# Gate and up of two feed-forward chunks as seven block products each, on one Trainium2 core

## The chip, the cores and the metric

The kernel runs on one core of one Trainium2 chip. The engines are named as the profile names them: PE (TensorE, matmul) with PEld (its weight loads), DVE (VectorE), ACT (ScalarE), POOL (GpSimd) and SP (SyncE, which issues the DMAs here). The metric is the device time of one execution in microseconds, less is better.

## The reference

Two layers, each with three sublayers (feed-forward, mixer, feed-forward), on 512 rows of 1024 channels. A modulation vector, one silu(c) @ ada_w per sublayer, shifts and scales the input of each sublayer and gates its output; a layer norm follows. Four of the six sublayers are the feed-forward network that the change touches:

```
def swiglu(h, w_gate, w_up, w_down):
    return (jax.nn.silu(h @ w_gate) * (h @ w_up)) @ w_down

def _ada_post_norm(x, mod, fn, ln_g, ln_b, res_w):
    shift, scale, gate = mod[:, 0, None], mod[:, 1, None], mod[:, 2, None]
    y = fn(x * (1 + scale) + shift)
    return layer_norm(DEEPNORM_ALPHA * x + res_w * (1 + gate) * y, ln_g, ln_b)
```

w_gate and w_up are 1024 x 2816, w_down is 2816 x 1024, all in 32-bit floating point.

## The kernel before

Channels lie on the 128 partitions, rows on the free axis: X, XH and XL are [128, 8, 512]. XH is the value rounded to the format of the matmul, XL the rest. Weights are split in the same way into a high and a low part, and each product of two values is three matmuls (high x high, high x low, low x high; `mm3`, L375 to L377).

Phases 0 to 5 are the sublayers: 0, 2, 3, 5 are feed-forward (FFN), 1 and 4 the mixers. An FFN works through its 2816 hidden channels in three chunks of 6, 8 and 8 tiles (`CHUNKS`). For each tile one **unit** is loaded: gate and up weights of 128 hidden channels, [128, 2, 8, 128], 1 MB. Gate and up are each 8 x 3 matmuls of 512 columns into one PSUM bank (PM, three banks). ACT takes silu out of PSUM (L644), DVE multiplies by up (L648), ACT casts the high part hH (L148), DVE forms the low part hL (L151). After a chunk's units comes its down stage: 8 output tiles, each evacuated by `resid` (L548, DVE), weights in four units. In chunks 0 and 1 it goes over all 512 columns; in chunk 2 (`last_projection`) first over one half of the columns for all output tiles, then over the other, and layer norm of the first half runs beside the second half of the products.

Units are handed through buffers. `load` fetches a unit into one of two raw buffers (SP). `halve` splits it in two steps, an ACT cast (L252) and, one piece later, a DVE subtraction (L255), into one of three buffers of the pool wp (tags wh, wl) or, for a few units, of the phase's own pool (tags dh, dl). `ready` lets a unit in only when the unit three before it (two for class d) has been marked done by `free`. `take` waits for a unit to be split and writes out what is still missing.

The order of work is written out by hand (`manual_schedule`): `run` emits a piece of matmuls with its evacuation, then `step` (what `after` has put off, as the DVE half of a split), then `tick`, which loads every fourth time, does a modulation sum every `ticks["ada"]` times, and else a halving on odd counts. Each engine executes its own queue in the order of emission. A modulation sum (`ada_sum`, L297) is one DVE operation over [128, 1024] after a 512 KB load into one of two aw buffers; there are 24 for each phase, 144 in all. `ADA_EVERY` sets their distance: one number for each phase, 3, 0, 6, 5, 0, 0. `ada_finish` does what is left of them and the small scalar operations (L322 to L334).

## Time and profile before

| | us |
|---|---|
| median of 3 runs | 1983.27 (1979.55 to 1985.62) |
| profiled execution, its own time | 1983.02 |
| its span, first to last instruction | 1981.2 |
| PE busy | 1950.2 |
| DVE busy | 1072.1 |
| ACT busy | 643.8 |

A row of the timeline gives the start, the duration, engine, line, operation, out<-in and shapes; a number in brackets is the idle time of the engine before it and what ended it. Matmuls overlap in their records, so the distance of two starts is what one costs. On DVE and ACT too an operation's record reaches some 0.08 us into the next one, so what one costs in a queue is again the distance of starts.

### The profile page before, as it was taken

What the parts mean: (1) busy time and instruction counts of PE and PEld (TensorE: products, weight loads), DVE (VectorE), ACT (ScalarE), POOL (GpSimd) and SP (SyncE); (2) the same over time, 40 slices, a digit from 0 to 9 for tenths busy, and PEclk for the clock granted to TensorE, in tenths of its full rate; (3) what the DMA queues carried; (4) which work ended last, traced back from release to release, by engine and by line L of the source; (5) the groups of instructions that cost most, each with busy time, mean ns of one, the idle gap of its engine ahead of it and who ended that gap; (6) DMA issues with size and microseconds to landing.
All of it is one profiled execution on the core that took longest, in us unless ns stands there. A gap on an engine that the chain in (4) does not pass through costs nothing.

```text
span 1981.2 us, 25603 instructions
## 1 busy us (share of the span) xinstructions
PE 1950.2 (98%) x10650; PEld 1659.7 (84%) x10650; DVE 1072.1 (54%) x1958; ACT 643.8 (32%) x966; POOL 0.3 (0%) x5
## 2 busy tenths in 40 slices
PE   7999999999999999999999999999999999999997
PEld 5888888988777998888899888888888998888887
DVE  7675654645356845545476545544795663333335
ACT  4322223253344532222335223122442352231221
POOL 0000000000000000000000000000000000000000
PEclk9999999999999999999999999999999999999998
DMA  9576652231141335444432554533122222323211
GB/s 340 199 266 231 212 191 92 75 107 64 54 138 65 112 123 181 154 165 149 160 127 85 174 188 160 180 107 128 65 86 85 86 96 97 107 85 106 86 64 43
DMA packets 57352, 259.18 MB, mean 131 GB/s; under 512 B 6083, under 2 KB 15724, under 8 KB 38549
## 3 DMA queue, kind: packets, MB, share of 16 engines
q1 hardware_dynamic: 57236, 257.56, 37.7%
q8 instruction: 83, 1.36, 0.3%
q14 instruction: 33, 0.26, 0.0%
HBM read 255.41 MB, written 2.12 MB: 130 GB/s over the span
## 4 chain that ended last, share of the span: by engine, by line
PE 94%; DVE 3%; DMA 1%; ACT 1%; issue 0%; SPq 0%; DVEq 0%; ACTq 0%
PE pm L375 30%; PE pm L376 29%; PE pm L377 29%; PE pa L1018 1%; PE pm L1042 1%; DMA aw<-in_adaw 1%; PE pb L485 1%; DVE aw L297 1%; PE pa L448 0%; ACT w L461 0%; PE pb L1029 0%; DVE wl L255 0%; PE pa L491 0%; DVE w L469 0%; DVE X L459 0%
## 5 line engine op out<-in xcount | busy, mean ns | idle before, releaser
L375 PE MATMUL pm<-XH,wh 128*128 128x512 f32 (+1 forms) x1656 | 619.0, 374 | 12.6 <-ACT wh L1306 11.6
L376 PE MATMUL pm<-XL,wh 128*128 128x512 f32 (+1 forms) x1656 | 614.5, 371 | 1.3 <-DVE XL L1354 1.3
L377 PE MATMUL pm<-XH,wl 128*128 128x512 f32 (+1 forms) x1656 | 614.2, 371 | 0.0
L255 DVE TENSOR_TENSOR wl<-raw,wh 128x1024 fp32r<-128x1024 f32 (+1 forms) x288 | 338.6, 1192 | 84.1 <-ACT wh L252 81.2
L252 ACT CAST wh<-raw 128x1024 fp32r<-128x1024 f32 (+1 forms) x288 | 285.0, 1024 | 280.4 <-PE pm L376 188.4
L375 PEld LDWEIGHTS pm<-XH,wh 128*128 128x128 f32 x1656 | 312.0, 188 | 73.5 <-ACT wh L1306 11.6
L376 PEld LDWEIGHTS pm<-XL,wh 128*128 128x128 f32 x1656 | 312.2, 189 | 60.1 <-DVE XL L1354 2.2
L377 PEld LDWEIGHTS pm<-XH,wl 128*128 128x128 f32 x1656 | 311.8, 188 | 59.4 <-DVE wl L1308 0.3
L648 DVE TENSOR_TENSOR w<-w,pm 128x512 f32<-128x512 f32 (+1 forms) x100 | 60.8, 608 | 382.4 <-PE pm L377 382.1
L376 PE MATMUL pm<-hL,wh 128*128 128x512 f32 (+1 forms) x704 | 250.8, 356 | 0.0
L375 PE MATMUL pm<-hH,wh 128*128 128x512 f32 (+1 forms) x704 | 250.2, 355 | 0.0
L377 PE MATMUL pm<-hH,wl 128*128 128x512 f32 (+1 forms) x704 | 247.7, 352 | 0.0
L548 DVE SCALAR_TENSOR_TENSOR X<-pm,sm,X 128x256 f32<-128x256 f32 (+1 forms) x176 | 101.4, 579 | 201.1 <-PE pm L377 201.1
L148 ACT CAST hH<-w 128x512 fp32r<-128x512 f32 (+1 forms) x103 | 57.6, 560 | 430.0 <-DVE w L648 430.0
L297 DVE CUSTOM_DVE_ANT_0 aw<-aw,sc_t,prm_t 128x1024 f32<-128x1024 f32 x144 | 183.6, 1280 | 24.2 <-DMA aw<-in_adaw 24.2
L375 PEld LDWEIGHTS pm<-hH,wh 128*128 128x128 f32 x704 | 132.2, 188 | 22.1
L377 PEld LDWEIGHTS pm<-hH,wl 128*128 128x128 f32 x704 | 132.4, 188 | 20.1
L376 PEld LDWEIGHTS pm<-hL,wh 128*128 128x128 f32 x704 | 132.4, 188 | 19.7
L644 ACT ACTIVATE w<-pm 128x512 f32<-128x512 f32 (+1 forms) x101 | 53.9, 534 | 202.1 <-PE pm L377 202.0
L151 DVE TENSOR_TENSOR hL<-w,hH 128x512 fp32r<-128x512 f32 (+1 forms) x103 | 63.3, 615 | 64.9 <-ACT hH L148 64.9
L375 PE MATMUL pm<-hH,dh 128*128 128x256 f32 x256 | 72.6, 284 | 0.0
L376 PE MATMUL pm<-hL,dh 128*128 128x256 f32 x256 | 72.4, 283 | 0.0
(239 smaller groups left out, 2143.0 us busy)
## 6 DMA issues: line engine op xcount, KB each, us to landing
raw<-in_wgu SPq DMA_DIRECT2D x84, 1024.0 KB, 4.9
aw<-in_adaw SPq DMA_DIRECT2D x144, 512.0 KB, 5.2
raw<-in_wd SPq DMA_DIRECT2D x32, 1024.0 KB, 5.0
raw<-in_wd SPq DMA_DIRECT2D x16, 768.0 KB, 4.2
raw<-in_abfm SPq DMA_DIRECT2D x8, 1024.0 KB, 4.8
raw<-in_cdfm SPq DMA_DIRECT2D x8, 1024.0 KB, 6.2
raw<-in_wgu SPq DMA_DIRECT2D x16, 256.0 KB, 8.9
raw<-in_abtm SPq DMA_DIRECT2D x4, 1024.0 KB, 4.9
```

The source lines that it names most:

```text
L148: A.copy(h, v)
L151: V.tensor_tensor(out=l, in0=v, in1=h.bitcast(F32), op=ALU.subtract)
L252: A.copy(u.hl[0][:, x], u.raw[:, x])
L255: V.tensor_tensor(out=u.hl[1][:, x], in0=u.raw[:, x], in1=u.hl[0][:, x].bitcast(F32), op=ALU.subtract)
L297: V.tensor_tensor_reduce(out=w, in0=w, in1=sc_t, scale=1.0, scalar=prm_t[:, c0:c0 + 1], op0=ALU.mult, op1=ALU.add, accum_out=mod[i][:, t:t ...
L375: T.matmul(ps, st[0], mv[0], start=first, stop=False)
L376: T.matmul(ps, st[0], mv[1], start=False, stop=False)
L377: T.matmul(ps, st[1], mv[0], start=False, stop=last)
L485: T.matmul(pv[t], q[:, n, t * P:(t + 1) * P], inv[:, 0:1], start=m + n == 0, stop=m == len(terms) - 1 and n == 1)
L548: V.scalar_tensor_tensor(out=X[:, d, cs], in0=ps, scalar=scal["G", i][:, d:d + 1], in1=X[:, d, cs], op0=ALU.mult, op1=ALU.add)
L644: A.activation(st["sg"], ps, AF.Silu)
L648: V.tensor_tensor(out=sg, in0=sg, in1=ps, op=ALU.mult)
```

## The change

In chunks 1 and 2 of each FFN, gate and up of a tile are computed together, as a product of 2 x 2 blocks with seven block products. The blocks are: of the weights, gate or up by the first or second four channel tiles (a11, a12, a21, a22); of the moving side, channel tiles 0 to 3 or 4 to 7 by the first or second 256 columns (HA, HB). Each block product is 4 x 3 matmuls of 256 columns. The products accumulate in three PSUM banks for each tile: product 1 is written to bank a and copied by ACT to bank b, in which product 2 adds to it; products 6, 7 and 4 add to bank a, with a copy or an addition taken out in between; product 5 is written to bank c, copied out, and product 3 adds to it. Product 4 of a tile is issued after products 1 and 5 of the next one. The two parts of ADA_EVERY, the waits and the buffers change with it:

- `quarter` takes the place of `halve` for these units: four sums and differences of weight blocks on DVE, four ACT casts, four DVE low parts; a unit takes two of the three wp buffers.
- `sums_of` forms the sums and differences of the moving blocks during the down stage of chunk 0, on DVE and ACT, into T23 and T4, which take the buffers of tags dh and dl until chunk 2's products are done, and over the second half of XH and XL for channel tiles 0 to 3.
- The down stage of chunk 2 keeps one unit of class d in place of two.
- Modulation sums: none in gate and up of chunks 1 and 2; every 4th tick in the down stage of chunk 0, every 2nd in those of chunks 1 and 2 (first half of columns); every 5th in the mixers. All later phases stand in one list from the start. `ada_finish` moves from before the first half of `last_projection` to behind it.

```
-ADA_EVERY = (3, 0, 6, 5, 0, 0)
+ADA_EVERY = {"up": (3, 0, 0, 0, 0, 0), "down": (4, 2, 2), "mixer": (0, 5, 0, 0, 5, 0)}
...
-                        add(wgu[f, j], [2, KT, P], "d" if j in ((3, 4) if i else (4,)) else "w", i)
+                        if c:
+                            add_seven(wgu[f, j], i)
+                        else:
+                            add(wgu[f, j], [2, KT, P], "d" if j in ((3, 4) if i else (4,)) else "w", i)
+                    if c == 0:
+                        hold(i)
                     for g in range(4):
-                        add(wd6[f, g] if n == 6 else wd8[f, c - 1, g], [2, n, P], "d" if c == 2 and g > 1 else "w", i)
+                        add(wd6[f, g] if n == 6 else wd8[f, c - 1, g], [2, n, P], "d" if c == 2 and g > 2 else "w", i)
...
+    def quarter(u):
+
+        sub = u.subs[u.n // 2]
+        if sub.hl is None:
+            if u.i not in sums_at or not ready(sub):
+                return False
+            sub.hl = tuple(wp.tile([P, 2, KT, P], F32R, tag="w" + x, name=nm("w" + x)) for x in "hl")
+        sr = sums_at[u.i]
+        a11, a12, a21, a22 = (u.raw[:, m, 4 * k:4 * k + 4, :] for m in range(2) for k in range(2))
+        if u.n == 0:
+            V.tensor_tensor(out=sr[:, 0], in0=a21, in1=a22, op=ALU.add)
+            V.tensor_tensor(out=sr[:, 1], in0=sr[:, 0], in1=a11, op=ALU.subtract)
+        elif u.n == 1:
+            V.tensor_tensor(out=sr[:, 2], in0=a11, in1=a21, op=ALU.subtract)
+            V.tensor_tensor(out=sr[:, 3], in0=a12, in1=sr[:, 1], op=ALU.subtract)
+        src = (u.raw[:, 0], sr[:, 0:2].rearrange("p a b c -> p (a b) c"), sr[:, 2:4].rearrange("p a b c -> p (a b) c"),
+               u.raw[:, 1, 4:8, :])[u.n]
+        h, l = (t[:, u.n % 2, 0:src.shape[1], :] for t in sub.hl)
+        u.n += 1
+        last = u.n == 4
+        A.copy(h, src)
+
+        def low():
+            V.tensor_tensor(out=l, in0=src, in1=h.bitcast(F32), op=ALU.subtract)
+            u.lows += 1
...
-        if ticks["n"] % 2 and halve():
+        if (eager or ticks["n"] % 2) and halve():
...
-        ada_finish(i + 1)
         zs = [W2([P, 2, HALF]) for _ in range(2)]
...
         for g in tiles(0):
             run(g)
+        ada_finish(i + 1)
...
+            def values():
+                for n in (k, k + 4):
+                    st[n] = W2()
+                    V.tensor_tensor(out=st[n], in0=XH[:, n, :].bitcast(F32), in1=XL[:, n, :].bitcast(F32), op=ALU.add)
+
+            def sums():
+                a, b = st[k], st[k + 4]
+                t, q = st["t"], st["q"] = W2([P, 2, HALF]), W2([P, 2, HALF])
+                V.tensor_tensor(out=q[:, 0], in0=a[:, HB], in1=a[:, HA], op=ALU.subtract)
+                V.tensor_tensor(out=t[:, 0], in0=b[:, HB], in1=q[:, 0], op=ALU.subtract)
+                V.tensor_tensor(out=t[:, 1], in0=b[:, HB], in1=a[:, HB], op=ALU.subtract)
+                V.tensor_tensor(out=q[:, 1], in0=b[:, HA], in1=t[:, 0], op=ALU.subtract)
+                A.copy(T23[0][:, k], t)
+                A.copy(XH[:, k, HB], q[:, 0])
+                A.copy(T4[:, 0, k], q[:, 1])
...
+                def e1(ps):
+                    A.copy(at("b")(), ps)
+
+                def e2(ps):
+                    t["g"] = W2()
+                    A.activation(t["g"][:, HA], ps, AF.Silu)
+                    free(u.subs[0])
+
+                def e3(ps):
+                    V.tensor_tensor(out=t["g"][:, HB], in0=t["u2"], in1=ps, op=ALU.add)
+                    A.activation(t["g"][:, HB], t["g"][:, HB], AF.Silu)
+
+                def e7(ps):
+                    t["c"] = W1()
+                    V.tensor_tensor(out=t["c"], in0=t["p5"], in1=ps, op=ALU.add)
+
+                def e4(ps):
+                    free(u.subs[1])
+                    g = t["g"]
+                    V.tensor_tensor(out=g[:, HA], in0=g[:, HA], in1=ps, op=ALU.mult)
+                    V.tensor_tensor(out=g[:, HB], in0=g[:, HB], in1=t["c"], op=ALU.mult)
+                    split(hH[:, jj, :], hL[:, jj, :], g)
...
+                p = unit(u, jj, (PM, PA)[jj % 2])
+                run([p[1], p[5]] + ([before[4]] if before else []) + [p[6], p[2], p[3], p[7]], eager=True)
+                before = p
+            run([before[4]], eager=True)
...
+            ticks["ada"] = ADA_EVERY["up"][i] if c == 0 else 0
+            if c:
+                seven(range(n), hH, hL)
+                jj = n
+                if c == len(CHUNKS) - 1:
+                    free(*held_d[i])
...
+                moving_sums = [f for k in range(4) for f in sums_of(k)]
...
+                        if c == 0:
+                            for f in moving_sums[3 * d // 2:3 * (d + 1) // 2]:
+                                after(1 + (d % 2), f)
```

## Rows read from the trace of the kernel before

**Rows 1.** The page's totals by engine, and TensorE's longest wait by who ended it: us in total, times, longest us.

```profile
PE 1950.2 (98%) x10650; PEld 1659.7 (84%) x10650; DVE 1072.1 (54%) x1958; ACT 643.8 (32%) x966; POOL 0.3 (0%) x5
...
PE pm L375 <- ACT wh L1306: 11.6, 1, 11.6
```

**Rows 2.** Busy time of each engine (instructions in brackets), granted clock, DMA share and GB/s in three stretches: gate and up of chunk 2 of the first FFN, the down stage of chunk 0 of the second FFN, and its down stage of chunk 2.

```profile
252.30:341.80 89.50, 89.50 (x389) 72.27 (x388) 40.20 (x48) 25.32 (x33) 0.00 (x0) 1.00 0.42 146
734.20:767.80 33.60, 33.60 (x146) 27.03 (x145) 19.74 (x25) 7.80 (x10) 0.00 (x0) 1.00 0.43 148
992.60:1041.00 48.40, 47.83 (x397) 47.55 (x397) 35.68 (x80) 15.93 (x24) 0.00 (x0) 1.00 0.36 122
```

**Rows 3.** Timeline of PE: the first and the seventh of a run of 512-column matmuls; the first and the thirteenth of a run of 256-column ones with weights in the pool of tag wh; the first and the tenth of a run with weights in that of tag dh.

```profile
303.10 0.39 PE L375 MATMUL pm<-XH,wh 128*128 128x512 f32 x1
304.50 0.39 PE L375 MATMUL pm<-XH,wh 128*128 128x512 f32 x1
...
705.93 0.28 PE L375 MATMUL pm<-XH,wh 128*128 128x256 f32 x1
707.29 0.28 PE L375 MATMUL pm<-XH,wh 128*128 128x256 f32 x1
...
690.02 0.28 PE L375 MATMUL pm<-XH,dh 128*128 128x256 f32 x1
691.10 0.29 PE L375 MATMUL pm<-XH,dh 128*128 128x256 f32 x1
```

**Rows 4.** Timeline, mostly of DVE, in several stretches: operations that follow each other without idle time, the end of a unit (last matmul, then the multiplication), and a pair of 512-wide additions of which the second reads the first.

```profile
208.06 0.69 DVE L151 TENSOR_TENSOR hL<-w,hH 128x512 fp32r<-128x512 f32 x1 [0.69 <-ACT hH L148]
208.67 1.28 DVE L297 CUSTOM_DVE_ANT_0 aw<-aw,sc_t,prm_t 128x1024 f32<-128x1024 f32 x1
...
733.85 0.40 PE L377 MATMUL pm<-XH,wl 128*128 128x512 f32 x1
734.36 0.69 DVE L648 TENSOR_TENSOR w<-w,pm 128x512 f32<-128x512 f32 x1 [7.46 <-PE pm L377]
...
764.37 1.22 DVE L255 TENSOR_TENSOR wl<-raw,wh 128x1024 fp32r<-128x1024 f32 x1
765.50 1.28 DVE L297 CUSTOM_DVE_ANT_0 aw<-aw,sc_t,prm_t 128x1024 f32<-128x1024 f32 x1
...
1046.69 1.42 DVE L469 TENSOR_TENSOR w<-w,w 128x512 f32<-128x512 f32 x2 [0.16 <-ACT w L461]
...
1061.96 0.75 DVE L510 TENSOR_TENSOR XL<-w,XH 128x256 fp32r<-128x256 f32 x2
```

**Rows 5.** Groups of instructions by line and shape, of ACT: busy us, mean ns of one, then idle time before them.

```profile
L252 ACT CAST wh<-raw 128x1024 fp32r<-128x1024 f32 x256 | 259.3, 1048 | 253.9 <-PE pm L376 188.4 <-issue 23.2 <-DMA raw<-in_wgu 19.9
L148 ACT CAST hH<-w 128x512 fp32r<-128x512 f32 x73 | 45.4, 622 | 380.2 <-DVE w L648 380.2
L644 ACT ACTIVATE w<-pm 128x256 f32<-128x256 f32 x30 | 11.5, 382 | 13.9 <-PE pm L377 13.8
```

**Rows 6.** The page's DMA issues: queue, count, KB each, median us from issue to landing.

```profile
raw<-in_wgu SPq DMA_DIRECT2D x84, 1024.0 KB, 4.9
aw<-in_adaw SPq DMA_DIRECT2D x144, 512.0 KB, 5.2
```

**Rows 7.** Timeline of DVE in the down stage of chunk 0 of the second FFN.

```profile
735.73 0.69 DVE L151 TENSOR_TENSOR hL<-w,hH 128x512 fp32r<-128x512 f32 x1 [0.69 <-ACT hH L148]
...
738.50 0.75 DVE L548 SCALAR_TENSOR_TENSOR X<-pm,sm,X 128x512 f32<-128x512 f32 x1 [1.07 <-PE pm L377]
739.17 0.95 DVE L255 TENSOR_TENSOR wl<-raw,wh 128x768 fp32r<-128x768 f32 x1
740.03 1.28 DVE L297 CUSTOM_DVE_ANT_0 aw<-aw,sc_t,prm_t 128x1024 f32<-128x1024 f32 x1
741.24 0.08 DVE L297 DVE_READ_ACCUMULATOR2_ANT mod<- 128x1 f32 x1
```

**Rows 8.** Timeline of DVE at the start of the down stage of chunk 0 of the first FFN, where PE begins at 83.28.

```profile
94.01 0.75 DVE L548 SCALAR_TENSOR_TENSOR X<-pm,sm,X 128x512 f32<-128x512 f32 x1
...
100.40 1.29 DVE L297 CUSTOM_DVE_ANT_0 aw<-aw,sc_t,prm_t 128x1024 f32<-128x1024 f32 x1 [2.05 <-DMA aw<-in_adaw]
...
106.80 1.28 DVE L297 CUSTOM_DVE_ANT_0 aw<-aw,sc_t,prm_t 128x1024 f32<-128x1024 f32 x1 [0.85 <-DMA aw<-in_adaw]
```

**Rows 9.** Timeline of PE at its start, and the table by stretches (columns as in rows 2) around its longest later wait, in the second mixer.

```profile
12.57 0.63 PE L377 MATMUL pm<-XH,wl 128*128 128x512 f32 x1
13.00 0.63 PE L375 MATMUL pm<-XH,wh 128*128 128x512 f32 x1
...
1424.00:1427.00 3.00, 0.99 (x9) 0.74 (x7) 2.81 (x5) 2.98 (x4) 0.00 (x0) 0.99 0.06 25
1427.00:1431.00 4.00, 4.00 (x13) 3.29 (x14) 3.68 (x19) 2.48 (x3) 0.00 (x0) 0.58 0.02 4
```

**Rows 10.** Timeline of DVE in the down stage of chunk 2 of the second FFN: the first evacuation of the second half, and the first operation of layer norm.

```profile
1017.82 0.48 DVE L548 SCALAR_TENSOR_TENSOR X<-pm,sm,X 128x256 f32<-128x256 f32 x1 [1.67 <-PE pm L377]
1018.68 2.48 DVE L459 TENSOR_TENSOR X<-X,pa 128x512 f32<-128x512 f32 x4 [0.38 <-PE pa L448]
```

**Rows 11.** Timeline of DVE at the start of the third FFN: the last low part of the first five units, and the multiplication of the fifth.

```profile
1064.78 1.22 DVE L255 TENSOR_TENSOR dl<-raw,dh 128x1024 fp32r<-128x1024 f32 x1
...
1071.48 0.42 DVE L648 TENSOR_TENSOR w<-w,pm 128x256 f32<-128x256 f32 x1 [2.24 <-PE pm L377]
```

More of the change, by code (lines that the diff above doesn't have):

```diff
@@ L163, in __init__ @@
             self.split = self.done = False
+            self.subs = None
+            self.n = self.lows = 0
     units = []
@@ L175, in add, with add_seven, hold @@
             members.setdefault((cls, i if cls != "w" else 0), []).append(u)
+        def add_seven(src, i):
+            u = Unit(src, [2, KT, P], "s", i)
+            u.subs = [Unit(None, u.shape, "w", i) for _ in range(2)]
+            units.append(u)
+            members.setdefault(("w", 0), []).extend(u.subs)
+        def hold(i):
+            held_d[i] = [Unit(None, None, "d", i) for _ in range(2)]
+            members.setdefault(("d", i), []).extend(held_d[i])
         for i in range(6):
@@ L261, in halve, with quarters @@
         return True
+    def quarter(u):
[21 more added lines that the diff above has]
+            u.lows += 1
+            if last:
+                u.split = True
+                halved[0] += 1
+        begun[0] += last
+        after(1, low)
+        return True
+    def quarters(u, n):
+        while u.lows < n:
+            if u.n >= n:
+                settle()
+            else:
+                assert load() or halve(), (used[0], halved[0], loaded[0], u.n)
     def prepare():
@@ L358, in tick, with run @@
             defer.pop(0)()
-    def run(pieces, extras=None, quiet=False):
+    def run(pieces, extras=None, quiet=False, eager=False):
         for n, p in enumerate(pieces):
@@ L366, in run @@
             if not quiet:
-                tick()
+                tick(eager)
     def flush(q):
@@ L632, in ffn, with sums_of, lows @@
         j0 = 0
+        T23 = T4 = None
+        def sums_of(k):
+            st = {}
+            def values():
[12 more added lines that the diff above has]
+                A.copy(T4[:, 0, k], q[:, 1])
+            def lows():
+                t, q = st["t"], st["q"]
+                for o, v, h in ((T23[1][:, k], t, T23[0][:, k]), (XL[:, k, HB], q[:, 0], XH[:, k, HB]),
+                                (T4[:, 1, k], q[:, 1], T4[:, 0, k])):
+                    V.tensor_tensor(out=o, in0=v, in1=h.bitcast(F32), op=ALU.subtract)
+            return values, sums, lows
@@ new lines, in seven, with product, piece, both @@
+        def seven(js, hH, hL):
+            def product(u, n, need, sub, w, ps, mv, first, evac):
+                def piece():
+                    quarters(u, need)
+                    h, l = u.subs[sub].hl
+                    ps_ = ps()
+                    for k in range(4):
+                        st_ = (h[:, w // 2, 4 * (w % 2) + k, :], l[:, w // 2, 4 * (w % 2) + k, :])
+                        m = mv(k)
+                        for x, (s_, v_) in enumerate(((st_[0], m[0]), (st_[0], m[1]), (st_[1], m[0]))):
+                            T.matmul(ps_, s_, v_, start=first and k + x == 0, stop=k == 3 and x == 2, skip_group_check=not first)
+                    evac(ps_)
+                return piece
+            def both(k, cs):
+                return XH[:, k, cs], XL[:, k, cs]
+            def unit(u, jj, bank):
+                b = {}
+                def at(n):
+                    def get():
+                        if n not in b:
+                            b[n] = bank([P, HALF])
+                        return b[n]
+                    return get
+                t = {}
+                def keep(n):
+                    def evac(ps):
+                        t[n] = W1()
+                        A.copy(t[n], ps)
+                    return evac
+                def e1(ps):
[16 more added lines that the diff above has]
+                    split(hH[:, jj, :], hL[:, jj, :], g)
+                p = {
+                    1: product(u, 1, 1, 0, 0, at("a"), lambda k: both(k, HA), True, e1),
+                    5: product(u, 5, 2, 0, 2, at("c"), lambda k: both(k, HB), True, keep("p5")),
+                    6: product(u, 6, 2, 0, 3, at("a"), lambda k: (T23[0][:, k, 0], T23[1][:, k, 0]), False, keep("u2")),
+                    2: product(u, 2, 1, 0, 1, at("b"), lambda k: both(4 + k, HA), False, e2),
+                    3: product(u, 3, 3, 1, 1, at("c"), lambda k: both(4 + k, HB), False, e3),
+                    7: product(u, 7, 3, 1, 0, at("a"), lambda k: (T23[0][:, k, 1], T23[1][:, k, 1]), False, e7),
+                    4: product(u, 4, 4, 1, 2, at("a"), lambda k: (T4[:, 0, k], T4[:, 1, k]), False, e4),
+                }
+                return p
+            before = None
+            for jj in js:
+                u = units[used[0]]
+                used[0] += 1
+                p = unit(u, jj, (PM, PA)[jj % 2])
+                run([p[1], p[5]] + ([before[4]] if before else []) + [p[6], p[2], p[3], p[7]], eager=True)
+                before = p
+            run([before[4]], eager=True)
@@ L1334, in start @@
         ada_q.extend((0, t) for t in range(16, 24))
-        ada_q.extend((n, t) for n in (1, 2) for t in range(24))
+        ada_q.extend((n, t) for n in range(1, 6) for t in range(24))
         def sums(k):
@@ L1385, in tile_kernel @@
             phase.update(i=i, pool=php)
-            ticks["ada"] = ADA_EVERY[i]
-            if i == 2:
-                ada_q.extend((n, t) for n in (3, 4, 5) for t in range(24))
+            ticks["ada"] = ADA_EVERY["up" if i in FFN_OF else "mixer"][i]
             if i == 1:
```

11 lines of the change are left out of this document (10 added, 1 removed).

## The prediction

> **What bounds the kernel now.** I read the page's totals and TensorE's waits first: TensorE (PE) is busy 1950.2 of 1981.2 us, and 11.6 of the 31 us left are one wait at the start [rows 1]. Time is to be won only by giving PE less to do, and is lost wherever PE is made to wait. Then the table by stage: a gate-and-up stage of eight units takes 89.5 us with PE busy throughout, VectorE (DVE) busy 40 and ScalarE (ACT) 25; eight such stages are changed [rows 2]. Then the spacing of matmul starts, since the ends are modelled: 512 columns cost 0.233 us (1.40 us for six), 256 columns with moving XH and weights from the pool of wh 0.1133 (1.36 for twelve), with weights from the pool of dh 0.120 [rows 3]. Last, DVE's order of work in the stages around, because DVE gets what PE is spared.
>
> **The seven products.** A unit is 48 matmuls of 512 columns, 11.19 us (89.5 / 8). It becomes 7 x 12 of 256 columns. Products 1, 5, 2, 3 move XH and XL: 1.36 us each. For 6, 7 and 4 the moving sums lie in the buffers of tag d; no row shows such a moving tile, the bounds are 0.1133 and 0.120, and I take 0.120 because that is what buffers there cost as weights: 1.44 us. PE's own time is 4 x 1.36 + 3 x 1.44 = 9.76 us, 1.43 less per unit, 91 us over 64.
>
> **DVE's chain per unit.** Starts in DVE's queue: 1024 elements 1.13 us (764.37 to 765.50), 512 elements 0.61 (208.06 to 208.67), 0.73 when an operation reads its predecessor's result (1.42 for a pair, less 0.69), 256 elements 0.335 (0.75 for two of 0.42) [rows 4]. ACT casts 1024 elements in 1.05 us, 512 in 0.62, and takes 256 out of PSUM in 0.38 [rows 5]. Before, a unit asks of DVE 2 x 1.13 + 0.69 + 0.61 = 3.6 us. After: four sums of 512 (2.5), low parts of 3 x 1024 and one 512 (4.0), four operations of 256 (1.35), the split (0.61): 8.5 us, in a fixed order. Let T be the end of product 4 of the unit before. The queue then holds: two multiplications (0.11 to begin, as 734.36 stands to the end of the matmul of 733.85, then 0.34, 0.42 to its end), the wait for ACT's 0.62 us cast (the same 0.69 us gap stands before every hL now), hL 0.61, first two weight sums 0.73 + 0.61, low part 1.13, two sums 1.22, low part 1.13, the add for product 3 0.34, low part 1.13, and the add for product 7, 0.42. Sum 8.9 us. Product 4 writes the bank that this last add reads, so it starts no sooner than T + 8.9. PE reaches it after products 6, 2, 3, 7, 1, 5 = 8.32 us, less 0.16 us by which the modelled end lags the slot: T + 8.2. So DVE, not PE, sets the period: 8.9 + 1.44 + 0.16 = 10.5 us, a PE wait of 0.7 in each full unit. ACT's copies of the unit (about 3.5 us of weights, 2.5 of the rest) fit beside it; the copy within PSUM is one 256-wide ACT operation, at most 0.38 us, two products ahead of its reader: nothing.
> A stage: product 4 of the first unit starts after 8.32 + 2.72 = 11.0 us, six more follow at 10.5 (74.0), the last takes 1.44. Four products (5.6) end at 81; the closing product 4 has no next unit between it and its add, which in addition is queued behind low parts of the down weights (their DMA starts when a raw buffer frees and lands 4.9 us later [rows 6]): about 1.5 us. Then 1.44: 84.2 us against 89.5. Eight stages: **-42 us** of the 91.
>
> **Down stage of chunk 0.** It now also makes the moving sums. PE takes 33.6 us [rows 2]. DVE is given: eight value sums 4.9, sixteen 256-wide 5.4, low parts 5.2, gaps for ACT's casts 1.4, eight evacuations 0.67 each 5.3, six modulation sums at 1.20 7.2, four low parts of 768 3.5, the first unit's weight sums and low parts 6.5: 39.4 us, against 20 now [rows 2, 7]. It starts 2.2 us late (the last hL), so its last evacuation ends near 41.6. Product 5 of the next unit takes that very PSUM bank, and product 6 needs the sums queued just before: PE, ready at 33.6 + 1.4 = 34.9, waits 6.8 us in the second and third FFN. In the first, DVE waits for landings of forced modulation sums and evacuates first at 94.01, 6.5 us late [rows 8]; the same list ends near 47: 12.5 us. In the last FFN no modulation sums are left (120 after the first, 30 in each of three FFNs, about 21 in the first mixer, 9 in the second): 0.6. Sum **+27** (bounds 0, if PE meets other work there, of which I see none, and 35).
> A wait of that length also costs clock. After the 11.6 us at the start PE runs 512 columns at 0.427 us, the 1.2 GHz level; after a 2 us wait in the second mixer the next 4 us show a granted 0.58 [rows 9]. Some 3.4 us at half speed lose about 1.6 us, three times: **+5** (0 to 8).
>
> **Modulation sums moved.** None in chunks 1 and 2; every second tick in their down stages. Tick distances are 2.8 us. With two aw buffers, sum n+2 can follow sum n by a landing plus 1.28; a load takes 5.2 us by the median [rows 6], and in the first FFN sums now wait 0.9 to 2 us for it, two of them in 6.4 us (100.40 to 106.80) [rows 8]. That rate does not sustain 2.8; undisturbed loads can be near 4. In chunk 1 DVE ends about 1.5 us behind PE's next product, three FFNs: **+4.5** (0 to 20). In chunk 2's first half, DVE gets four low parts of down weights, eight modulation sums, eight evacuations in 23 us, then the scalar operations (now behind them): the sum over channels is late, and PE's queue holds the mean's matmul early in the second half, with layer norm's chain behind it, which today begins 0.86 us after the first evacuation of that half [rows 10]. I take 3.8, 2.5 and 1.7 us: **+8** (0 to 20). In the mixers, modulation loads now pass SP's queue between bias loads, and 30 sums of 1.2 us DVE's; the filler covers nearly all: **+1** (0 to 6).
>
> **Buffers at the start of a phase.** Chunk 2 keeps three down units in the w pool instead of two, so the next phase's first unit cannot be halved until the first of them is freed, in the second half. Everything prepared slips by two or three halves. In the third FFN's start the low parts of the first five units now end with the one at 1064.78 [rows 11]; with the slip, the first half of unit 4 follows the evacuation of unit 3: done near 1071, where PE, whose unit 4 of 5.8 us ends just before 1071.48, wants it at 1065.6. I take 6 us there, 1.5 and 2 in the two mixers that follow an FFN: **+9.5** (2 to 15).
>
> **The sum.** -42 + 27 + 5 + 4.5 + 8 + 1 + 9.5 = +13 us. The profiled execution took 1983.0 us (span 1981.2 and 1.8 around it), next to the median of 1983.27: **1996 us**.
>
> **Rivals.**
> Faster, 1958: the per-unit wait vanishes. DVE has 8.5 us of work per 9.76; if the add for product 7 reached DVE by T + 8.2, the 0.7 us in 48 full units (34) and half of the closing waits would go: 1996 - 38. It decides at that point. For it: only 0.7 us are missing and some of DVE's starts may overlap better. Against it: the queue is in order, and every duration has its row.
> Faster, 1964: DVE's load at the first boundary costs nothing, because its excess of 6 us is worked off behind products that need none of it: 1996 - 32. Against it: product 5 waits for a bank.
> Slower, 2020: the modulation loads land late (5 to 6 us, as now in the first FFN). Sixteen sums at 3.3 us are 53 us against 44.8 (eight outputs of 24 matmuls at 0.233), eight are 27 against 23; beyond what I took, some 8 us for each of three FFNs: 1996 + 24.
> Slower, 2040: the clock. The Trainium skill, TensorE: Matmul & The Clock Gate, "A second HAM failure mode: psum-queue depth-cycling", says that small idle times between matmul groups, as PSUM banks are cycled, can keep the clock swinging between its levels. Here a stretch with waits of 0.57 us kept 1.00 [rows 2], which speaks against it. As a mechanism of this kernel: the 0.7 us waits would bring half speed to some units; 84 x 0.2135 (half of 0.427) is 17.9 us in place of 10.5, and one unit in ten gives 6 x 7.4 = +44.
>
> **How the numbers follow.** Forecast as walked (1978 to 2012) 0.50; per-unit wait gone 0.20; boundary hidden 0.13; modulation loads late 0.15; clock 0.02. A measurement can tell 0.3%, 6 us, from no change: 1977 to 1989 is "same". The forecast's own range gives 0.02 below, 0.14 within, 0.34 above. Faster 0.33 + 0.02 = 0.35; same 0.14 and 0.02 from rivals half realised, 0.16; slower 0.34 + 0.17 less those 0.02 = 0.49. The range 1955 to 2018 leaves out some 0.1 on either side: both faster rivals together, and the worst of the loads or the clock. The forecast alone: 1978 to 2012.
>
> **What would show it.** In the changed kernel: starts of product 1 of successive units 10.5 us apart (9.8 would be the first rival), with PE idle before product 4 released by the add for product 7; 256-wide spacings of 0.113 and 0.120; a PE wait of about 7 us, 12 in the first FFN, before the second product of chunk 1, released by the last evacuation; none in the last FFN; granted 0.5 behind it; DVE waiting for aw in down stages of chunks 1 and 2; PE waiting at the mean's matmul and at unit 4 of the third FFN. I am wrong if the products run at another spacing, or if DVE's order differs from the one I read out of the program.

## The result, and the profile after

The changed kernel takes 1999.6 us (median of 4 runs, 1997.5 to 2001.7) against 1983.0 (1979.6 to 1985.6): ratio 1.0085, 95% interval 1.0066 to 1.0104, slower by 16.6 us. The profiled execution took 1997.5, its span is 1995.8 us against 1981.2. Answers to [rows 1], the totals and TensorE's longest waits:

```profile
PE 1893.8 (95%) x12954; PEld 1725.5 (86%) x12954; DVE 1446.8 (72%) x2678; ACT 831.2 (42%) x1398; POOL 0.3 (0%) x5
...
PE pm L740 <- DVE X L614: 26.4, 6, 7.4
PE pa L740 <- DVE w L779: 18.8, 32, 2.3
PE pm L441 <- ACT wh L1496: 11.5, 1, 11.5
PE pm L740 <- DVE w L779: 8.8, 24, 0.4
PE pb L551 <- DVE w L535: 4.8, 5, 1.5
```

PE works 56 us less and ends 15 us later: it waits. L740 is the matmul of the seven products. Nearly all its waits are of two kinds: for the evacuation L614 of the down stage (6 waits, up to 7.4 us) and, in every unit, for the add for product 7 (L779).

The table by stretches, as in [rows 2]: chunk 2 of the last FFN, where nothing disturbs the stage; the down stage of chunk 0 of the second FFN, which now also makes the moving sums; and its down stage of chunk 2.

```profile
1844.70:1928.80 84.10, 80.78 (x674) 79.25 (x673) 66.67 (x98) 45.91 (x79) 0.00 (x0) 1.00 0.28 98
745.95:779.55 33.60, 33.60 (x145) 27.03 (x144) 31.46 (x54) 10.73 (x18) 0.00 (x0) 1.00 0.37 125
1003.70:1054.90 51.20, 49.09 (x402) 48.34 (x401) 41.28 (x90) 15.81 (x24) 0.00 (x0) 1.00 0.45 155
```

DVE is busy 66.7 of 84.1 us in a stage, and 31.5 of 33.6 us in the down stage of chunk 0 without being done by its end. Answers to [rows 3], the spacing of PE's starts: the first and the fourth matmul with moving XH, the first and the seventh with moving th.

```profile
779.56 0.28 PE L740 MATMUL pm<-XH,wh 128*128 128x256 f32 x1
779.90 0.28 PE L740 MATMUL pm<-XH,wh 128*128 128x256 f32 x1
...
1882.40 0.28 PE L740 MATMUL pa<-th,wh 128*128 128x256 f32 x1
1883.10 0.28 PE L740 MATMUL pa<-th,wh 128*128 128x256 f32 x1
```

0.34 / 3 = 0.113 and 0.70 / 6 = 0.117 us. DVE in a unit (answers to [rows 4]), from the multiplication after one product 4 (L784) to the next; left out are the other weight sums and the low parts of the first two quarters:

```profile
823.25 0.42 DVE L784 TENSOR_TENSOR w<-w,pm 128x256 f32<-128x256 f32 x1 [1.19 <-PE pm L740]
823.59 0.42 DVE L785 TENSOR_TENSOR w<-w,w 128x256 f32<-128x256 f32 x1
824.69 0.69 DVE L153 TENSOR_TENSOR hL<-w,hH 128x512 fp32r<-128x512 f32 x1 [0.69 <-ACT hH L150]
825.31 0.68 DVE L299 TENSOR_TENSOR sr<-raw 128x512 f32<-128x512 f32 x1
...
830.11 0.41 DVE L774 TENSOR_TENSOR w<-w,pa 128x256 f32<-128x256 f32 x1
830.44 1.22 DVE L312 TENSOR_TENSOR wl<-sr,wh 128x1024 fp32r<-128x1024 f32 x1
831.57 0.41 DVE L779 TENSOR_TENSOR w<-w,pa 128x256 f32<-128x256 f32 x1
831.90 0.68 DVE L312 TENSOR_TENSOR wl<-raw,wh 128x512 fp32r<-128x512 f32 x1
833.78 0.42 DVE L784 TENSOR_TENSOR w<-w,pa 128x256 f32<-128x256 f32 x1 [1.19 <-PE pa L740]
```

From 823.25 to the next such multiplication at 833.78 are 10.53 us. The add for product 7 (L779) starts 8.3 us into the unit, with the third quarter's low part (L312, 1.22) just ahead of it; behind it DVE is idle for 1.19 us, since it needs the result of product 4, which waited for it. The record shows PE idle for only some 0.37 us at that point, since the ends are modelled; the period says 0.76 (10.53 less the 9.77 that PE needs, shown below).

Where the 14.6 us of span came from, by stage. A stage goes from its first matmul in the timeline of PE to the first of the next; of the experiments below, three stand beside.

| us | before | after | boundary sums out | down units in d | all edits |
|---|---|---|---|---|---|
| first FFN: down of chunk 0 | 33.6 | 39.5 | 37.2 | 39.5 | 37.2 |
| gate and up 1 and 2 | 89.6, 89.6 | 93.3, 90.1 | 91.8, 89.0 | 93.6, 88.7 | 87.7, 85.2 |
| down of chunk 2 | 49.2 | 51.4 | 52.5 | 57.4 | 51.2 |
| second FFN: gate and up 1 and 2 | 89.6, 89.6 | 94.0, 85.3 | 85.6, 87.7 | 93.5, 85.4 | 81.0, 81.8 |
| down of chunk 2 | 49.1 | 51.2 | 50.9 | 51.4 | 49.3 |
| third FFN: start to down of chunk 0 | 69.5 | 78.5 | 77.9 | 69.4 | 69.7 |
| gate and up 1 and 2 | 89.6, 89.6 | 93.3, 84.9 | 85.8, 84.4 | 93.8, 84.8 | 82.7, 79.9 |
| down of chunk 2 | 48.2 | 49.5 | 49.3 | 49.1 | 48.3 |
| second mixer to down of chunk 0 | 240.3 | 241.1 | 242.9 | 242.5 | 241.1 |
| last FFN: gate and up 1 and 2 | 89.6, 89.6 | 85.6, 84.1 | 85.6, 84.1 | 85.8, 84.1 | 81.0, 79.6 |

The boundary of chunk 0 and 1 in the second FFN: DVE ends its list for the down stage at 787.60 with the last evacuation, 8 us behind PE's last down matmul (779.33); ahead of it stand a modulation sum (L363) and, for one pair of channel tiles, the four operations that make the moving sums and their three low parts (the last one is shown).

```profile
783.21 1.28 DVE L363 CUSTOM_DVE_ANT_0 aw<-aw,sc_t,prm_t 128x1024 f32<-128x1024 f32 x1
...
787.26 0.42 DVE L727 TENSOR_TENSOR th<-w,th 128x256 fp32r<-128x256 f32 x1
787.60 0.75 DVE L614 SCALAR_TENSOR_TENSOR X<-pm,sm,X 128x512 f32<-128x512 f32 x1
...
788.49 0.55 PE L740 MATMUL pm<-XH,wh 128*128 128x256 f32 x1 [7.41 <-DVE X L614]
788.84 0.41 PE L740 MATMUL pm<-XL,wh 128*128 128x256 f32 x1
789.05 0.41 PE L740 MATMUL pm<-XH,wl 128*128 128x256 f32 x1
```

Product 5 starts 7.41 us late and its matmuls then stand 0.21 us apart (788.84 to 789.05) in place of 0.113. The table by stretches shows why: the column of the granted clock (third from the right) is at 0.50 there, the lower of its two levels, 1.2 GHz. It falls again at the start of the third FFN, the place of [rows 11], behind waits of 0.8 to 1.9 us (last line):

```profile
784.00:788.00 4.00, 0.00 (x0) 0.00 (x0) 3.62 (x10) 2.33 (x5) 0.00 (x0) 0.50 0.88 311
788.00:792.00 4.00, 3.51 (x16) 3.54 (x17) 3.97 (x6) 0.72 (x3) 0.00 (x0) 0.50 0.20 82
792.00:796.00 4.00, 4.00 (x31) 4.00 (x30) 1.23 (x2) 1.81 (x4) 0.00 (x0) 0.81 0.00 0
...
1086.00:1090.00 4.00, 3.37 (x17) 3.38 (x18) 1.71 (x2) 0.26 (x1) 0.00 (x0) 0.64 0.21 65
```

### The profile page after: what moved, and what is told of

The parts are those of the page before. It is cut to its first block, busy times and chain, and to the rows that moved or that the text cites. A ratio compares the mean times of both kernels' runs of the same rounds, so it can differ in the third digit from the quotient of the medians.

```text
span 1995.8 us, 31326 instructions
## 1 busy us (share of the span) xinstructions
PE 1893.8 (95%) x12954; PEld 1725.5 (86%) x12954; DVE 1446.8 (72%) x2678; ACT 831.2 (42%) x1398; POOL 0.3 (0%) x5
## 4 chain that ended last, share of the span: by engine, by line
PE 51%; DVE 36%; DMA 6%; ACT 4%; issue 2%; SPq 0%; DVEq 0%; ACTq 0%
PE pm L441 12%; PE pm L443 12%; PE pm L442 12%; DVE wl L312 9%; PE pm L740 6%; DMA aw<-in_adaw 5%; DVE aw L363 4%; PE pa L740 4%; DVE wl L281 3%; DVE sr L300 2%; DVE hL L153 2%; ACT hH L150 2%; DVE sr L303 2%; DVE sr L299 2%; DVE sr L302 2%
## 5 line engine op out<-in xcount | busy, mean ns | idle before, releaser
L281 DVE TENSOR_TENSOR wl<-raw,wh 128x1024 fp32r<-128x1024 f32 (+1 forms) x168 | 194.5, 1170 | 44.8 <-ACT wh L278 44.2
L363 DVE CUSTOM_DVE_ANT_0 aw<-aw,sc_t,prm_t 128x1024 f32<-128x1024 f32 x144 | 183.4, 1280 | 58.0 <-DMA aw<-in_adaw 57.6
L441 PE MATMUL pm<-XH,wh 128*128 128x256 f32 (+1 forms) x632 | 213.5, 338 | 12.6 <-ACT wh L1496 11.5
L442 PE MATMUL pm<-XL,wh 128*128 128x256 f32 (+1 forms) x632 | 209.4, 331 | 1.6 <-DVE XL L1544 1.5
L443 PE MATMUL pm<-XH,wl 128*128 128x256 f32 (+1 forms) x632 | 208.8, 330 | 0.0
L278 ACT CAST wh<-raw 128x1024 fp32r<-128x1024 f32 (+1 forms) x168 | 164.9, 1002 | 48.2 <-PE pm L442 38.8
L740 PE MATMUL pm<-XH,wh 128*128 128x256 f32 x512 | 145.4, 284 | 29.3 <-DVE X L614 26.4
L614 DVE SCALAR_TENSOR_TENSOR X<-pm,sm,X 128x256 f32<-128x256 f32 (+1 forms) x176 | 101.3, 577 | 77.1 <-PE pm L443 77.1
L312 DVE TENSOR_TENSOR wl<-sr,wh 128x1024 fp32r<-128x1024 f32 x128 | 155.9, 1218 | 1.7 <-ACT wh L309 1.5
L740 PE MATMUL pm<-XH,wl 128*128 128x256 f32 x512 | 146.5, 286 | 0.0
L740 PE MATMUL pa<-XH,wl 128*128 128x256 f32 x512 | 144.4, 282 | 0.0
L740 PE MATMUL pm<-XL,wh 128*128 128x256 f32 x512 | 144.4, 282 | 0.0
L441 PEld LDWEIGHTS pm<-XH,wh 128*128 128x128 f32 x632 | 119.0, 188 | 26.9 <-ACT wh L1496 11.5
L740 PE MATMUL pa<-XH,wh 128*128 128x256 f32 x512 | 142.2, 278 | 0.0
```

Of the source, the lines that this page charges most:

```text
L278: A.copy(u.hl[0][:, x], u.raw[:, x])
L281: V.tensor_tensor(out=u.hl[1][:, x], in0=u.raw[:, x], in1=u.hl[0][:, x].bitcast(F32), op=ALU.subtract)
L312: V.tensor_tensor(out=l, in0=src, in1=h.bitcast(F32), op=ALU.subtract)
L363: V.tensor_tensor_reduce(out=w, in0=w, in1=sc_t, scale=1.0, scalar=prm_t[:, c0:c0 + 1], op0=ALU.mult, op1=ALU.add, accum_out=mod[i][:, t:t ...
L441: T.matmul(ps, st[0], mv[0], start=first, stop=False)
L442: T.matmul(ps, st[0], mv[1], start=False, stop=False)
```

## The experiments

All start from the changed kernel; medians and ratios are against the kernel before, and gains are told against the 1999.6 us of the kernel after.

**The low part of the third quarter, one piece later.** In `quarter`:

```
-        after(1, low)
+        after(2 if u.n == 3 else 1, low)
```

> In the stages of seven products the low part of the third quarter of the next unit's weights stands in VectorE's queue between the add for product 3 and the add for product 7; here it is put one piece later, behind the add for product 7. Nothing else is changed. Theory (the order of VectorE's queue sets the period, 10.53 us): the chain from the end of one product 4 to the add for product 7 is 1.13 us shorter, the wait of TensorE before product 4 goes in the 48 full units, units stand 9.8 us apart, 34 us less: 1966 us. Rival one (TensorE pays the wait for coming back to a bank that VectorE reads, whatever the order): the period stays 10.5 and the time 2000. Rival two (VectorE's total work is the bound): the moved low part is then in the way of the two multiplications after product 4; the period becomes 10.1 to 10.2, the time 1980 to 1985.

Measured: 1973.3 us, ratio 0.9947 (0.9928 to 0.9966), 26 us gained. One moved instruction turns a kernel 0.8% slower than the one before into one 0.5% faster. Units are 9.88 to 9.97 us apart. DVE's queue at the same place:

```profile
1858.60 0.41 DVE L774 TENSOR_TENSOR w<-w,pa 128x256 f32<-128x256 f32 x1
1858.93 0.41 DVE L779 TENSOR_TENSOR w<-w,pa 128x256 f32<-128x256 f32 x1
1859.26 1.22 DVE L312 TENSOR_TENSOR wl<-sr,wh 128x1024 fp32r<-128x1024 f32 x1
1860.40 0.68 DVE L312 TENSOR_TENSOR wl<-raw,wh 128x512 fp32r<-128x512 f32 x1
1861.62 0.42 DVE L784 TENSOR_TENSOR w<-w,pa 128x256 f32<-128x256 f32 x1 [0.54 <-PE pa L740]
```

The add (L779) now follows the one for product 3 directly, and the low parts lie in the time in which DVE had been idle. This settles what set the period; the rivals (the way back to the bank, DVE's whole work) would have left 10.5 or 10.2. The gain is less than the 34 us forecast because units stop at 9.9, not 9.8, and the closing product 4 waits a little longer (1.3 in place of 1.1). Part of that is a slower pace of PE itself: seven of the eight stages go over to 9.97 after two to five units, and there no matmul waits, they merely stand further apart (last section).

**Product 1 kept in SBUF, product 2 in a bank of its own, added on DVE.**

```
-                    A.copy(at("b")(), ps)
+                    t["p1"] = W1()
+                    A.copy(t["p1"], ps)
...
-                    A.activation(t["g"][:, HA], ps, AF.Silu)
+                    V.tensor_tensor(out=t["g"][:, HA], in0=t["p1"], in1=ps, op=ALU.add)
+                    A.activation(t["g"][:, HA], t["g"][:, HA], AF.Silu)
...
-at("b"), lambda k: both(4 + k, HA), False, e2)
+at("b"), lambda k: both(4 + k, HA), True, e2)
```

> The copy within PSUM is undone: product 1 is kept in SBUF (ScalarE, as for product 5), product 2 starts its bank anew, and VectorE adds the two ahead of silu. Theory (VectorE's queue up to the add for product 7 sets the period): one 256-wide add more stands in that chain, 0.34 us; units 10.87 us apart in place of 10.53, 48 x 0.34 = +16: 2016 us. Rival (PE's own time or the return to the bank sets the period): 2000. Should the copy cost something today, it would be faster: 1990.

Measured: 2014.7 us, ratio 1.0159 (1.0144 to 1.0175), 15 us lost; units are 10.91 us apart. The copy within PSUM saves an add in the one place where 0.34 us of DVE are 0.38 us of time; a price of its own doesn't show.

**Both together.**

> Both edits: product 1 kept in SBUF with one more add on VectorE, and the low part of the third quarter put behind the add for product 7. Theory: with the late low part the chain is some 8.1 us against the 8.2 to 8.3 at which TensorE comes to product 4, so the added 0.34 us lies in slack: units 9.9 us apart as with the late low part alone, 1973 to 1978 us. Rival (VectorE's whole work counts, not only what stands ahead of that add; it is then 9.6 us of 9.9): units 10.2 apart, 1973 + 16 = 1989.

Measured: 1981.6 us, ratio 0.9990 (0.9979 to 1.0001): 8 us behind the late low part alone, units 10.21 us apart. The period is the rival's, the time lies between the two, and the mechanism is not the rival's: DVE is still idle for 0.54 us and then 0.69 in each unit. PE now waits earlier, in product 5:

```profile
1327.33 1.22 DVE L312 TENSOR_TENSOR wl<-sr,wh 128x1024 fp32r<-128x1024 f32 x1
...
1328.18 0.28 PE L740 MATMUL pa<-XL,wh 128*128 128x256 f32 x1
1328.60 0.38 PE L740 MATMUL pa<-XH,wl 128*128 128x256 f32 x1
```

The low part of the second quarter (begun at 1327.33) ends at 1328.55, and the first matmul that reads it (XH,wl) starts at 1328.60, 0.31 us later than its spacing of 0.113 would have it. My theory looked only at the add for product 7; the next link of the same chain lay 0.1 us behind it.

**hL two pieces later, with the late low part.**

```
-                    split(hH[:, jj, :], hL[:, jj, :], g)
+                    split(hH[:, jj, :], hL[:, jj, :], g, 2)
```

> The late low part of the third quarter, and in addition hL is put two pieces later in VectorE's queue, behind the next unit's first two weight sums, so that the 0.69 us in which VectorE waits for ScalarE's cast is filled. Theory (with the late low part alone the next link is the second quarter's low part, which TensorE reaches at product 5 some 0.1 us too early: units 9.88 to 9.97 apart against 9.76 of its own): that link comes 0.7 us earlier, units stand 9.76 to 9.8 apart, 56 x 0.1 to 0.15 us, 6 to 8 us off the 1973 us of the late low part: 1966 us. Rival (9.88 to 9.97 is TensorE's own pace): 1973. Should hL be late for the down stage, the waits there eat the gain: 1973 or more.

Measured: 1964.9 us, ratio 0.9903 (0.9884 to 0.9923). Units stand 9.77 us apart in seven of the eight stages, which is PE's own time as the prediction worked it out (9.76), and 9.97 in one:

```profile
824.22 0.42 DVE L784 TENSOR_TENSOR w<-w,pa 128x256 f32<-128x256 f32 x1 [1.21 <-PE pa L740]
...
833.99 0.42 DVE L784 TENSOR_TENSOR w<-w,pm 128x256 f32<-128x256 f32 x1 [1.21 <-PE pm L740]
```

So the link at product 5 was what held 9.88. The 9.97 is a pace of PE's own, as the rival has it, but it sets in behind the stall at that same link (last section), and of the seven stages that had it six are rid of it now. In the late-low run some 27 units stood 9.97 apart; at 0.20 us each they are about 5 us, most of the 8 gained.

**A modulation sum in about every unit.**

```
-            ticks["ada"] = ADA_EVERY["up"][i] if c == 0 else 0
+            ticks["ada"] = 7 if c else ADA_EVERY["up"][i]
```

> Every 7th tick of the stages of seven products also takes a modulation sum, about one per unit, as long as there are sums left (about 32 in the first and second FFN; from the third FFN on next to none are left anywhere). Theory (VectorE's chain has no room, so its every operation lengthens the period): units with a sum stand 11.7 to 11.8 us apart in place of 10.5, 32 x 1.2 = +38 us; the third FFN, without sums, loses its wait of 7.4 us at the first product of chunk 1 and the clock behind it, about -12, and other down stages some -3: 2023 us. Rival (the wait before product 4 is not VectorE's work, which has 1.2 us idle per unit): the period stays 10.5 and only the gain is left, 1985.

Measured: 2030.5 us, ratio 1.0238 (1.0223 to 1.0254). I had counted that next to no sums would be left for the third FFN; five still stood in its down stage of chunk 0, so its wait of 7.4 us stayed, about as much as the 7.5 us by which the expectation missed. The stages tell more than the sum. With ten, eleven, nine and nine sums, the first two stages of the first FFN and those of the second have units 11.42, 11.73, 10.53 and 11.42 us apart. In the third of these the sums cost nothing:

```profile
855.71 0.41 DVE L779 TENSOR_TENSOR w<-w,pa 128x256 f32<-128x256 f32 x1
856.04 0.68 DVE L312 TENSOR_TENSOR wl<-raw,wh 128x512 fp32r<-128x512 f32 x1
856.64 1.28 DVE L363 CUSTOM_DVE_ANT_0 aw<-aw,sc_t,prm_t 128x1024 f32<-128x1024 f32 x1
857.85 0.08 DVE L363 DVE_READ_ACCUMULATOR2_ANT mod<- 128x1 f32 x1
857.92 0.42 DVE L784 TENSOR_TENSOR w<-w,pa 128x256 f32<-128x256 f32 x1
...
980.75 1.28 DVE L363 CUSTOM_DVE_ANT_0 aw<-aw,sc_t,prm_t 128x1024 f32<-128x1024 f32 x1
```

At 856.64 the sum stands behind the add for product 7, in the 1.2 us that DVE is idle; at 980.75 it stands ahead of the weight sums, inside the chain, and costs 0.9; ahead of the add itself (11.73) it costs 1.2. "Every operation lengthens the period" was wrong: its place decides.

**Modulation sums out of the down stage of chunk 0.**

```
-"up": (3, 0, 0, 0, 0, 0), "down": (4, 2, 2),
+"up": (3, 0, 4, 4, 0, 0), "down": (0, 2, 2),
...
-            ticks["ada"] = ADA_EVERY["down"][c]
+            ticks["ada"] = ADA_EVERY["down"][c] or (8 if i == 0 else 0)
```

> No modulation sums in the down stage of chunk 0 of the second and third FFN (6 each before), every 8th tick instead of every 4th in the first FFN; every 4th tick of chunk 0's gate and up in the second and third FFN takes them in their place. Theory (VectorE's excess of work in that stage makes TensorE wait at the second product of chunk 1): the waits of 7.4 us in the second and third FFN fall to 1.2 or less, as in the last FFN, and 11.7 in the first to about 8; the half-clock spells behind them go or shrink (some 8 us of loss): 2000 - 12.4 - 3.7 - 8 = 1976 us. Rival (the wait is the chain of the moving sums through ScalarE's copies, not the load of VectorE): the waits stay near 7 and the time at 1996 to 2000.

Measured: 1981.5 us, ratio 0.9989 (0.9979 to 0.9998), 18 us gained. The wait of the second FFN:

```profile
778.80 0.36 PE L740 MATMUL pm<-XH,wh 128*128 128x256 f32 x1 [1.23 <-DVE X L614]
```

7.41 became 1.23, in the third FFN too, the last FFN's value. The two stages lose 8.5 and 7.5 us, of which 6.2 are the wait; the other 2.3 and 1.3 are matmuls that no longer run at half clock (granted 1.00 in both stages now). The first FFN's wait of 7.0 us fell to 5.0 only, and its down stage stays 3.6 us too long: landings of the sums forced there come on top. The total stays 5.5 us above the 1976 expected: besides the first FFN, chunk 2 of the second took 2.4 us more than in the kernel after and the second mixer 1.8, and the cause of these two is open.

**The third down unit back in tag d,** each unit of the last projection completed when it is reached:

```
-"d" if c == 2 and g > 2 else "w"
+"d" if c == 2 and g > 1 else "w"
...
-                us = take(4)
+                us = units[used[0]:used[0] + 4]
+                used[0] += 4
+
+                def ops(d, k, cs):
+                    complete(us[d // 2])
+                    return operands(us[d // 2], d, k, cs)
```

> The third down unit of chunk 2 goes back from the pool of wh to the buffers of tag d, as before the change, and the last projection asks for each unit only when it comes to it. Theory (the next phase's first units are halved late because three down units of chunk 2 hold the pool of wh): the waits at the start of the third FFN (4.4 us and two half-clock spells) and of the two mixers (0.5 and 4.3) go, 8 us of waits and some 4 of clock: 1988 us. Rival one (these waits come from the modulation sums and loads that now stand in the second down stage): no change, 1999. Rival two (two units that may only be halved once the last moving sums are read bring VectorE four low parts in the first half of the last projection): waits of 1 to 3 us there in each FFN, 2003.

Measured: 1994.5 us, ratio 1.0055 (1.0037 to 1.0074), 5 us gained; the interval overlaps with that of the kernel after, so the stages have to decide. The start of the third FFN is at 69.4 us again, as before the change, with no wait left: 9.0 us, 4.4 of them recorded waits, 3.4 lost clock (counted below), the rest not assigned. Rival two is also right, in the first FFN alone: its last down stage grew by 6 us, where PE waits 4.0 for layer norm. Ahead of layer norm in DVE's queue stand the late low parts, but also modulation sums that wait 2.1 and 2.8 us for their landings; the share of each isn't shown.

**No modulation sums in the last down stages.**

```
-            ticks["ada"] = ADA_EVERY["down"][c]
+            ticks["ada"] = 0 if i and c == 2 else ADA_EVERY["down"][c]
```

> No modulation sums in the down stage of chunk 2 of the second and third FFN (8 each); the list then lasts longer and nothing else is moved. Theory (the moved sums delay the sum over channels, so TensorE waits for layer norm): those two down stages, now 51.2 and 49.5 us, go back to 49.0 and 48.2 as before the change: 1996 us. Rival (the late low parts of the down weights delay it): no change, 1999 to 2000.

Measured: 2019.5 us, ratio 1.0192 (1.0164 to 1.0220). The two stages did as the theory says: 51.2 to 49.0 and 49.5 to 48.9 us (one sum was left in it). But the sums left over are due by the end of the second mixer, and were forced there one landing after the other; PE waits for layer norm's chain:

```profile
PE pb L551 <- DVE w L535: 21.9, 4, 19.1
```

The stretch from the third FFN's end to the last FFN's down stage went from 241.1 to 263.8 us. So the expected total is missed by 23 us, for a reason that is neither theory: I had not counted whether the list still came to its end in time.

**Matmuls that nobody reads, in the waits at the boundary**, once in each of the first three FFNs:

```
+            filler_on[0] = c == 1
...
+                    if jj == 0 and len(js) == 8 and i != 5 and filler_on[0]:
+                        filler_on[0] = False
+                        d_ = PB([P, HALF])
+                        for _ in range(54):
+                            T.matmul(d_, u.subs[0].hl[0][:, 0, 0, :], XH[:, 0, HA], start=True, stop=True)
```

> The kernel after the change, with 54 matmuls of 256 columns more, whose result nobody reads, behind the first product of chunk 1 in the first three FFNs, where TensorE waits 7.0 to 7.4 us; 54 x 0.113 = 6.1 us lie within each wait. Theory (the half-clock matmuls behind such a wait follow from TensorE having stood idle): the granted clock stays at 1.00 behind the filled waits, and gate and up of chunk 1 lose what they have above their waits, about 2 us each (93.3, 94.0 and 93.3 us to some 91.3, 91.7 and 91.5): 1994 us. Rival (the clock falls whatever TensorE does there): stages and time as they are, 1999 to 2000.

Measured: 1995.9 us, ratio 1.0066 (1.0048 to 1.0083). Against the kernel after the intervals overlap, so the time alone decides nothing; the clock and the stages do. The same stretches as above:

```profile
784.00:788.00 4.00, 3.26 (x29) 3.06 (x28) 3.62 (x10) 2.28 (x5) 0.00 (x0) 1.00 0.85 295
788.00:792.00 4.00, 3.45 (x29) 3.48 (x30) 3.96 (x7) 1.85 (x4) 0.00 (x0) 1.00 0.25 98
792.00:796.00 4.00, 4.00 (x37) 4.00 (x37) 2.72 (x5) 2.30 (x5) 0.00 (x0) 1.00 0.01 2
```

The granted clock stays 1.00, and this stage and the third FFN's fall from 94.0 to 91.9 and from 93.3 to 91.8, as forecast: PE's idle time is the cause of the half clock, at 1.5 to 2.1 us for a wait of 7.4. In the first FFN the clock stayed up behind the filled wait too, yet its stage did not gain (93.7): its closing product 4 waited 2.2 us in place of 1.15, and behind that the granted clock fell (0.66 from 212 to 217), which cost 1.4. Why it waited longer was not found.

**All edits.** A first combination (late low part, sums out of the down stages of chunks 0 and 2, tag d in the second FFN alone):

> Together: the low part of the third quarter behind the add for product 7; modulation sums kept out of the down stages of chunks 0 and 2 of the second and third FFN (every 8th tick in the first FFN's chunk 0), every 4th tick of gate and up of chunk 0 there instead; the third down unit of chunk 2 back in tag d in the second FFN alone. If the causes are separate, their gains add up: from 2000, 26 for the late low part, 16 for the two boundaries, 4 for the first FFN, 9 for the start of the third FFN, 2 to 3 for layer norm: 1942 us, ahead of both kernels. If they share a cause (one wait only taking another's place) less than half of that beyond the late low part: 1960 or more.

Measured: 1962.4 us, ratio 0.9895 (0.9880 to 0.9910), 20 us above the sum of the gains, with the same forced sums as above: 19.0 us of wait at the end of the second mixer. With the sums spread so that they end in time, and hL later:

```
-ADA_EVERY = {"up": (3, 0, 0, 0, 0, 0), "down": (4, 2, 2), "mixer": (0, 5, 0, 0, 5, 0)}
+ADA_EVERY = {"up": (3, 0, 3, 3, 0, 0), "down": (0, 2, 0), "mixer": (0, 5, 0, 0, 4, 0)}
...
-            ticks["ada"] = ADA_EVERY["down"][c]
+            ticks["ada"] = (8, 2, 2)[c] if i == 0 else ADA_EVERY["down"][c]
...
-"d" if c == 2 and g > 2 else "w"
+"d" if c == 2 and g > (1 if i == 2 else 2) else "w"
```

> As in the combined run before, with the modulation sums spread so that none is left to be forced at the end of the second mixer (every 3rd tick of gate and up of chunk 0 in the second and third FFN, every 4th in the second mixer), and with hL two pieces later. Theory: the phase of the second mixer loses the 24 us that it had gained in the combined run (265 back to 241 us): 1962 - 24 = 1938, and with hL as in its own run 1932 to 1938. Rival (the sums still miss their time, or delay something else): 1945 or more.

Measured: 1932.1 us, ratio 0.9750 (0.9725 to 0.9775): 2.5% faster than the kernel before, 67 us less than after. PE is busy 1868 of 1929.0 us:

```profile
PE 1868.2 (97%) x12954; PEld 1712.9 (89%) x12954; DVE 1443.2 (75%) x2678; ACT 828.0 (43%) x1398; POOL 0.3 (0%) x5
```

## Why the prediction was right, point by point

The forecast, 1996 us, is 3.6 us from the median; its terms stand against the profile as follows. A stage without disturbance takes 84.11 us; what a stage has beyond that and its waits is counted to the clock, as a remainder.

| us | forecast | after |
|---|---|---|
| eight stages without disturbance, 8 x (84.1 - 89.6) | -42 | -43.8 |
| boundary of chunk 0 and 1: 12.9, 7.4, 7.4, 1.2 | +27 | +28.9 |
| clock behind waits: 2.1 + 3.0 + 2.5 + 1.8, and 4.6 in the third FFN | +5 | +14.0 |
| modulation loads in chunk 1 (3.0 + 0 + 0.3) and a late closing product (1.1) | +4.5 | +4.4 |
| layer norm: 2.2 + 2.2 + 1.2 | +8 | +5.6 |
| mixers: -0.3 in the first | +1 | -0.3 |
| buffers at the start of a phase: 4.4, and 0.9 before the last FFN | +9.5 | +5.3 |
| sum (of the spans: 14.6) | +13 | +14.1 |

The clock can also be counted directly, as PE's busy time times the lost share of the granted clock: in the lines above, 3.51 x 0.50 + 4.00 x 0.19 = 2.5 us for the second FFN. So counted the five places of the clock's row lose 1.8, 3.0, 2.5, 1.7 and 3.4 us, 12.4 of the 14.0. The kernel before had two such spells in its mixers, one of them in [rows 9], 1.7 us each; the kernel after has none there. They are hidden in its -0.3 and 0.9 for the mixers, and net of them the clock costs 9 us.

- **DVE's chain per unit** held: 10.53 us against 10.5, PE's own 9.77 against 9.76, and the late low part alone gave back 26 us. The first rival (1958, the wait vanishes) put its price at 38 us; with hL later 35 came back, by edits that the change did not make. The modulation rival (2020) did not come: in the down stage of chunk 1 of the second and third FFN 15 sums each went through without making it longer (44.8 us), and landings of these loads have a median of 4.1 us now, 5.2 before [rows 6].
- **The boundary** held in size and place, and the second rival (1964) is out: the excess is DVE's load, as the run without those sums shows.
- **The clock** is the term that was mis-sized, and its bounds (0 to 8) missed it, by either count of what the kernel after loses. I charged it to three waits of the boundary, which cost 2.1, 2.5 and 1.8. What I left out are the waits of 1 to 3 us: one of 3.0 us cost 3.0 more in chunk 2 of the first FFN, and those at the start of the third FFN 3.4 (4.6 as a remainder). [Rows 9] had such a case, 0.58 behind a wait of 2 us, and I used it for the long waits alone. That it didn't move the total is luck: layer norm and buffers were put 7 us too high.
- Three sums of the prediction don't come out as printed: the terms of a stage give 84.0 us (printed 84.2, so -44 over eight, and -43.8 came), the wait in the first FFN 12.1 (12.5), the price of the first rival 40 (38). None of them moves the forecast by more than 2 us.
- The clock rival (2040) is refuted as a mechanism: in chunk 2 of the last FFN, with a wait in every unit, the granted clock is 1.00. The Trainium skill, TensorE: Matmul & The Clock Gate, "A second HAM failure mode: psum-queue depth-cycling", says that small gaps as banks are cycled can make the clock swing; this stage does not show it.

## What to carry to other kernels

When one engine gets what another is spared, write its queue out for one period and mark the operation that the other engine waits for: only what stands ahead of that counts, and an operation that nobody waits for yet belongs behind it. Look for the second link before trusting the first: here the next one lay 0.1 us behind. Work moved out of a crowded stage has to fit where it goes and still end before its due time; count it to the end of the list.

## What was not expected of the hardware

The same sequence of 84 matmuls, out of the same buffers and with the granted clock at 1.00, took 9.77 us per unit in seven stages of one run and 9.97 in the eighth, for all its units. In the slower one 256 columns with moving XH stand 0.118 us apart throughout, in the others 0.113 after the first few behind a product that moves th. The run with the late low part alone shows where the slower pace begins. In all seven of its stages that go over to it, it sets in inside product 5, behind the stall at the second quarter's low part (801.42 to 801.63), and then stays for the rest of the stage:

```profile
801.31 0.28 PE L740 MATMUL pm<-XL,wh 128*128 128x256 f32 x1
801.42 0.37 PE L740 MATMUL pm<-XH,wl 128*128 128x256 f32 x1
801.63 0.28 PE L740 MATMUL pm<-XH,wh 128*128 128x256 f32 x1
...
802.57 0.28 PE L740 MATMUL pm<-XH,wl 128*128 128x256 f32 x1
```

From 801.63 on the starts are 0.94 / 8 = 0.118 us apart. In the eighth stage the same stall comes in unit after unit and the pace falls back to 0.113 within a few matmuls; in the kernel after, the wait before product 4 ends it in every unit that has that wait. What decides between the two was not found; the slower pace is worth 1.6 us a stage.

Short waits do not always cost clock. At the start of the third FFN the kernel after shows waits of PE of 1.0, 0.8, 1.9 and 0.8 us, and the one with filled waits the same and one more of 0.8. Behind the last two the granted clock was 0.64 in the one (1086 to 1090, above) and 1.00 in the other:

```profile
1082.00:1086.00 4.00, 3.81 (x31) 3.81 (x32) 1.27 (x2) 0.39 (x1) 0.00 (x0) 1.00 0.36 115
```

The start took 78.5 us in the one and 76.2 in the other. What decides that stays open, and with it the size of the clock term for waits of 1 to 3 us; for 7.4 us it is shown.
